# A decoder block on one core: when the last phase's weights are split, where its gate is applied, and where the head sums stand

## The chip, the core and the metric

The kernel runs on 1 core of one Trainium2 chip, in one launch. The metric is the device time of one execution in microseconds. The core has a matrix engine (TensorE, PE in the profile, with its weight loads as PEld), a vector engine (VectorE, DVE), a scalar engine (ScalarE, ACT), a general engine (GpSimd, POOL), and SyncE (SP), which here only issues transfers. Each engine works through its own queue in order. Transfers are issued from SP's queue (q1 in the profile) and from GpSimd's (q0), and run on sixteen DMA engines.

## What is computed

One decoder block with two parallel token mixers, over 2048 tokens of width 1024, all in float32:

```python
mod = silu(c) @ ada_w + ada_b                       # shift, scale, gate: 1024 each
h = rmsnorm(x, norm_g) * (1 + scale) + shift
p = h @ w_in                                        # 1024 -> 9344 columns
# branch A: GLU, causal depthwise convolution of width 31, layer norm over channels, swish
u = layernorm(conv(val * sigmoid(gate_c)), ln_g, ln_b)
y_conv = (silu(u) * silu(og_c)) @ w_conv_out
# branch B: RWKV-7 time mixing, 16 heads of 64
#   state = state * w - (state @ kk) kk*a + v k ;  o = state @ r
o = layernorm_per_head(o) + sum_head(r * k * r_k) * v
y_rwkv = (o * silu(og_r)) @ w_rwkv_out
m = sigmoid(g_conv) * y_conv + sigmoid(g_rwkv) * y_rwkv
x = x + gate * (m @ w_out)
return rmsnorm(x, final_g)
```

Three things of it bear on the change. `gate` multiplies a column of `m @ w_out`, so it can as well multiply that column of `w_out`. The layer norm needs one variance per token. And `sum_head(r * k * r_k)`, one number per token and head, is needed only when it multiplies `v`.

## The kernel before

**Blocks and phases.** The 2048 tokens are four blocks of 512. The first phase goes through them in order (loop `for b in range(NB)`, which builds `h`, the four `group`s, and the work between): the input projection, the convolution and the recurrence, whose results go to scratch in HBM. The last phase (the second loop over `b`) does the three output projections and the final norm. In the profile the first phase reaches until about 2570 us.

**Float32 by three products.** A float32 factor is split into a part `hi` in the format `F32R` and a rest `lo`. A projection is three matmuls per tile of 128 rows: `hi*hi`, `hi*lo`, `lo*hi` (`mm3k`, L173, and `part`, L1023 to L1025, for `w_out`).

**Weights.** `load_w` brings a weight tile of 128 x 1024 (512 KB) into a ring of six buffers, tag `w`. If `kept` holds the tile, two loads from GpSimd's queue fetch `hi` and `lo` from HBM scratch (L149, L150). Otherwise SP loads the tile (`w_st`, L153), ScalarE copies it to `hi` (L156) and VectorE or GpSimd subtracts (`lo`, L158). Only the tiles of `w_in` are stored back to be kept (`KEPT`), in block 0; blocks 1 to 3 load them split. The 24 tiles of `w_rwkv_out` (`ro`), `w_conv_out` (`co`) and `w_out` (`o`) are needed once in each block of the last phase, so they are split 96 times. There the rule of L157 gives every subtraction to VectorE.

**A group of the first phase.** `group(b, g, ...)` does four heads, as two `pair`s. A pair projects `k`, `r` and `v` (`shifted`), builds decay products, and forms the masked score tiles `As` (L504 on TensorE, L506 on VectorE). The tile `rk = r * k * r_k` is made on VectorE (L487); ScalarE copies its `hi` part (`rh`, L490), GpSimd subtracts the rest (`headsum`, L248), two matmuls sum it over the head (L249, L250), and ScalarE copies the sum back into `rk` (L492). All this stands ahead of the score tiles. `v` is projected after them, transposed (L519), and multiplied by `rk` on GpSimd (L522). Both `pv` and `pb` come from one ring of two PSUM buffers, tag `aux`. After both pairs comes a small inverse on GpSimd (L568, L570), fed by transfers `dA` and `dT` in SP's queue, and then the recurrence over eight chunks (L642 to L667). `fill` puts convolution and gate projections between. A scheduler that works on a model of the machine orders the instructions of each engine, by priority and program order; `tc.high_priority(HP)` raises a priority.

**The x buffers.** `hx(name)` gives a 128 x 512 buffer from a ring of four, tag `hx`. The next block's normalisation (`xnorm`), the loads of `h` (`hprep`, `hf`), and in block 3 the first block's layer norm and products (`lnorm_first`, `z_first`) use them.

**The gate.** In block 0, after group 0, `hgate_col` is filled: the gate, one column per 128 channels, times `0.5 * D`. Ahead of the last phase's loop, L986 to L992 turn it into rows: `grow`, the gate along the free axis in all 128 partitions, by eight diagonal tiles and matmuls against `ones` (which holds 1/1024).

**The last phase.** Block 0's branch projections (`rproj`, `cproj`) run beside the last recurrence. In the loop, block `b` has `cproj(b)`; then for the next block `osplit` (three loads, two products on GpSimd, a split) and `lnorm`; then the output projection, four column blocks `cb` of 256; then `rproj(b + 1)`. `lnorm` sums over channels with `ones` on TensorE, so that mean and variance stand in all 128 partitions (128 x 512); L969 and the nine steps of `rsqrt` (L123 to L128) work on that on VectorE, and GpSimd multiplies by it (L977). `addx` takes the products out of PSUM: VectorE multiplies by `grow` (`tg`, L1030), GpSimd adds to `x` (L1034; VectorE at the very end), ScalarE squares and sums (L1036). `finish` normalises and stores.

## Time and profile before

| | us |
|---|---|
| median of 3 runs | 3218.7 |
| lowest, highest | 3214.45, 3227.28 |
| the profiled execution | 3226.71 |
| its span, first to last instruction | 3225.0 |

The profile shows one execution. Busy time is that of an engine's own instructions; its share is of the span. "Idle before" in a row is the time in which the engine sat idle just before such an instruction, and behind `<-` stands what ended it. A window's row gives busy time and count of each engine, the clock that TensorE was granted (1.00 is full), the mean busy share of the sixteen DMA engines, and what they moved in GB/s. Matmuls are pipelined, so that a row's mean duration is longer than the distance from one to the next.

### The profile page before, as it was taken

To read this page: it belongs to the slowest core of one execution; us is meant where nothing else is said; L and a number is where in the kernel's file an instruction comes from. 1 tells how busy PE (TensorE), PEld (TensorE's weight loads), DVE (VectorE), ACT (ScalarE), POOL (GpSimd) and SP (SyncE) were. 2 spreads that over 40 slices of the span, in tenths; PEclk is the share of its full clock that TensorE was granted. 3 is DMA by queue.
4 is the path that set the end of the run, shared out by engine and by line. 5 is a ranking of instruction groups with operands and counts; after the bars stand their busy time and mean duration, and the time that the engine had idled before them with its cause. 6 is when DMAs were issued, how large, how long until landed. Compare 5 with 4: busy or idle time off the path is not lost.

```text
span 3225.0 us, 64867 instructions
## 1 busy us (share of the span) xinstructions
PE 3040.3 (94%) x25664; PEld 2832.5 (88%) x25664; DVE 2305.3 (71%) x4328; ACT 1062.0 (33%) x1900; POOL 1386.1 (43%) x2158
## 2 busy tenths in 40 slices
PE   6899999999999999899999998999989998688998
PEld 5899998989999999799999998999979888577887
DVE  6787777866676767575867676767788357999755
ACT  4432525241414132313232332222232323343422
POOL 3264444534343434343444435535546315655201
PEclk9999999999999999899999998999989999899999
DMA  7766666755565556364646676646537656655553
GB/s 292 260 238 226 229 218 244 230 176 157 161 185 157 168 179 192 113 186 145 191 151 184 185 217 183 196 134 193 158 108 242 206 183 203 219 177 182 171 166 121
DMA packets 328464, 606.95 MB, mean 188 GB/s; under 512 B 130848, under 2 KB 147552, under 8 KB 328160
## 3 DMA queue, kind: packets, MB, share of 16 engines
q1 hardware_dynamic: 265088, 373.14, 35.4%
q0 software_dynamic: 63072, 229.67, 23.2%
q8 instruction: 202, 3.31, 0.4%
q14 instruction: 102, 0.84, 0.1%
HBM read 439.03 MB, written 162.53 MB: 187 GB/s over the span
## 4 chain that ended last, share of the span: by engine, by line
PE 69%; DVE 14%; DMA 8%; issue 3%; POOL 3%; ACT 3%; SPq 1%; DVEq 0%; POOLq 0%; ACTq 0%
PE ps_main L173 47%; PE aux L504 3%; DMA w_st<-w_in_t 3%; PE xo L656 2%; PE xo L647 2%; PE xo L627 2%; PE xo L642 2%; PE pout L1024 2%; PE xo L662 2%; PE pout L1023 2%; PE pout L1025 2%; DVE acc L733 1%; DMA As<-dT 1%; ACT w_hi L156 1%; PE late L609 1%
## 5 line engine op out<-in xcount | busy, mean ns | idle before, releaser
L173 PE MATMUL ps_main<-h_hi,w_hi 128*128 128x256 f32 x4608 | 976.1, 289 | 15.3 <-DVE carry L401 9.1
L173 PE MATMUL ps_main<-h_lo,w_hi 128*128 128x256 f32 x4608 | 969.4, 287 | 0.2 <-DVE h_lo L328 0.2
L173 PE MATMUL ps_main<-h_hi,w_lo 128*128 128x256 f32 x4608 | 964.3, 287 | 3.2 <-POOL w_lo L158 3.0
L173 PEld LDWEIGHTS ps_main<-h_hi,w_hi 128*128 128x128 f32 x4608 | 725.8, 191 | 31.1 <-DVE carry L401 8.9
L173 PEld LDWEIGHTS ps_main<-h_lo,w_hi 128*128 128x128 f32 x4608 | 727.2, 191 | 9.4 <-issue 3.7
L173 PEld LDWEIGHTS ps_main<-h_hi,w_lo 128*128 128x128 f32 x4608 | 723.5, 191 | 13.1 <-POOL w_lo L158 4.0
L733 DVE SCALAR_TENSOR_TENSOR acc<-u,ck,acc 128x512 f32<-128x512 f32 x928 | 697.9, 752 | 23.5
L149 POOL DMA_DIRECT2D w_hi<-kh_in x219 | 126.2, 576 | 526.6 <-PE ps_main L173 497.0
L156 ACT CAST w_hi<-w_st 128x1024 fp32r<-128x1024 f32 x167 | 175.1, 1048 | 400.9 <-DMA w_st<-w_in_t 125.3
L158 DVE TENSOR_TENSOR w_lo<-w_st,w_hi 128x1024 fp32r<-128x1024 f32 x120 | 164.9, 1374 | 115.1 <-PE ps_main L173 45.2
L568 POOL TENSOR_TENSOR itmp<-La,TT 128x126 f32<-128x126 f32 (+22 forms) x496 | 181.0, 365 | 107.8 <-DMA La<-dA 75.4
L667 DVE SCALAR_TENSOR_TENSOR S<-xo,pe,Se 64x64 f32<-64x64 f32 x512 | 144.7, 283 | 93.1 <-PE xo L662 82.7
L637 ACT ACTIVATE Se<-S,pe 128x128 f32<-128x128 f32 x256 | 89.1, 395 | 357.9 <-DVE S L667 357.6
L570 POOL TENSOR_TENSOR TT<-TT,itmp 128x126 f32<-128x126 f32 (+22 forms) x496 | 189.6, 382 | 34.1
L506 DVE TENSOR_TENSOR As<-aux,maskA 128x512 f32<-128x512 f32 x128 | 88.1, 690 | 143.4 <-PE aux L504 142.7
L158 POOL TENSOR_TENSOR w_lo<-w_st,w_hi 128x1024 fp32r<-128x1024 f32 x47 | 112.9, 2401 | 112.9 <-ACT w_hi L156 89.2
L1034 POOL TENSOR_TENSOR xt<-xt,tg 128x256 f32<-128x256 f32 x60 | 55.5, 946 | 199.0 <-DVE tg L1030 196.5
L658 DVE TENSOR_TENSOR uv<-xo,rn 64x256 f32<-64x256 f32 x128 | 53.8, 421 | 120.5 <-PE xo L656 119.7
L504 PE MATMUL aux<-KR,BKz 128*128 128x128 f32 x1024 | 133.9, 277 | 1.9 <-DVE As L506 1.1
L522 POOL TENSOR_TENSOR vv<-rk,vv 128x512 f32<-128x512 f32 x32 | 45.0, 1407 | 197.5 <-PE aux L519 117.3
L504 PEld LDWEIGHTS aux<-KR,BKz 128*128 128x128 f32 x1024 | 123.7, 191 | 4.6 <-DVE As L506 1.8
L150 POOL DMA_DIRECT2D w_lo<-kl_in x219 | 119.3, 545 | 18.9 <-PE ps_main L173 11.1
(294 smaller groups left out, 5726.4 us busy)
## 6 DMA issues: line engine op xcount, KB each, us to landing
w_hi<-kh_in POOLq DMA_DIRECT2D x219, 512.0 KB, 4.1
w_lo<-kl_in POOLq DMA_DIRECT2D x219, 512.0 KB, 5.2
w_st<-w_in_t SPq DMA_DIRECT2D x73, 512.0 KB, 4.9
kh_in<-w_hi SPq DMA_DIRECT2D x71, 512.0 KB, 3.0
kl_in<-w_lo SPq DMA_DIRECT2D x71, 512.0 KB, 4.5
w_st<-w_ro_t SPq DMA_DIRECT2D x32, 512.0 KB, 4.1
w_st<-w_co_t SPq DMA_DIRECT2D x32, 512.0 KB, 3.6
w_st<-w_o_t SPq DMA_DIRECT2D x32, 512.0 KB, 3.6
```

Of the source, the lines that this page charges most:

```text
L149: nc.gpsimd.dma_start(hi, back[0])
L150: nc.gpsimd.dma_start(lo, back[1])
L156: nc.scalar.copy(hi, st)
L158: lo_eng.tensor_tensor(out=lo, in0=st, in1=hi.bitcast(F32), op=ALU.subtract)
L173: nc.tensor.matmul(ps[:, qs], ww[:, k, :], aa[k][:, qs], start=(k == 0 and t == 0 and q == 0), stop=(k == KT - 1 and t == 2 and q == ms - ...
L504: nc.tensor.matmul(pA[:, c // 2, es], BKz[:, hh, cc, es], KR[:, cc, es], start=(c == 0), stop=(c == 3), skip_group_check=True)
L506: nc.vector.tensor_tensor(out=Asb[:, hh, c4 * 4:c4 * 4 + 4, :].rearrange("p (a e) n -> p a (e n)", e=2), in0=pA, in1=flat(maskA).unsqueeze ...
L568: nc.gpsimd.tensor_tensor(out=tmp[:, :ni, :nt], in0=La[:, j:j + 1, j + 1:].broadcast_to([P, ni, nt]), in1=TT[:, :ni, j:j + 1].broadcast_to ...
L570: nc.gpsimd.tensor_tensor(out=TT[:, :ni, j + 1:], in0=TT[:, :ni, j + 1:], in1=tmp[:, :ni, :nt], op=ALU.add)
L637: nc.scalar.mul(Se[:, q, :], Sg[:, q, :], R[q]["pe"][:, c:c + 1])
L667: nc.vector.scalar_tensor_tensor(out=Sg[hs, q, hs], in0=xo[hs, 2 + q, hs], scalar=R[q]["pe"][hs, c:c + 1], in1=Se[hs, q, hs], op0=ALU.mult ...
L733: nc.vector.scalar_tensor_tensor(out=acc if i + 1 < HALO else yj, in0=u[:, i:i + TB], scalar=ck[:, j, i:i + 1], in1=acc, op0=ALU.mult, op1 ...
```

## The change

Five edits. (1) The 24 tiles of `ro`, `co` and `o` are split once, in halves of 128 x 512, behind the groups of blocks 1 and 2, three tiles to a group; the halves use the x buffers, the subtraction is GpSimd's, and both parts are stored in HBM scratch. In the last phase `load_w` then finds every tile kept. (2) The gate, times 0.5 alone, is stored to HBM as a row, and its 256 columns multiply a half of `o` before that is split; `grow`, its matmuls and the product in `addx` are gone, and `addx` is one addition on VectorE per token tile. (3) `lnorm` computes the variance with the tokens in the partitions, 128 x 4; `rsqrt` works on that, and four diagonal tiles and one matmul spread the result to 128 x 512. (4) In `pair` the head sums stand behind the transposes of `v`. (5) The two multiplications that take a branch projection out of PSUM, and the addition in `addx`, get the raised priority.

```diff
+    grow_d = dp.tile([D], F32, name="grow_d", tag="grow_d")
+    later = [(n, j) for n in ("ro", "co") for j in range(KT)] + [("o", (cb, kh)) for cb in range(4) for kh in range(2)]
...
+    def presplit(name, n, half):
...
+        hs = slice(half * 4, half * 4 + 4)
+        st, hi, lo = hx("w_st"), hx("w_hi"), hx("w_lo")
+        nc.sync.dma_start(st.rearrange("p (k n) -> p k n", k=4), wsrc[name][n][:, hs, :])
+        if name == "o":
+            gr = hx("w_gr")
+            nc.sync.dma_start(gr[:, :256], grow_d[n[0] * 256:n[0] * 256 + 256].unsqueeze(0).broadcast_to([P, 256]))
+            s4 = st.rearrange("p (k n) -> p k n", n=256)
+            nc.gpsimd.tensor_tensor(out=s4, in0=s4, in1=gr[:, :256].unsqueeze(1).broadcast_to([P, 2, 256]), op=ALU.mult)
+        nc.scalar.copy(hi.bitcast(F32R), st)
+        nc.gpsimd.tensor_tensor(out=lo.bitcast(F32R), in0=st, in1=hi, op=ALU.subtract)
+        for d_, s_ in zip(back, (hi, lo)):
+            nc.sync.dma_start(d_[:, hs, :].bitcast(F32), s_.rearrange("p (k n) -> p k n", k=4))
...
@@ pair
-        pb = pa.tile([P, TB], F32, name="aux", tag="aux")
-        rh = e1.tile([P, TB], F32R, name="rh", tag=RHT)
-        nc.scalar.copy(rh, rk)
-        headsum(pb, rk, rh)
-        nc.scalar.copy(rk, pb)
         yield
...
         for e in range(2):
             nc.scalar.copy(uv[vrow(e), e::2, q_, :], pv[vrow(e)])
+        pb = pa.tile([P, TB], F32, name="aux", tag="aux")
+        rh = e1.tile([P, TB], F32R, name="rh", tag=RHT)
+        nc.scalar.copy(rh, rk)
+        headsum(pb, rk, rh)
+        nc.scalar.copy(rk, pb)
         nc.gpsimd.tensor_tensor(out=vv, in0=rk, in1=vv, op=ALU.mult)
...
@@ first phase, behind a group
-                nc.vector.tensor_scalar(out=hgate_col, in0=hgate_col, scalar1=0.5 * D, scalar2=None, op0=ALU.mult)
+                nc.vector.tensor_scalar(out=hgate_col, in0=hgate_col, scalar1=0.5, scalar2=None, op0=ALU.mult)
+                nc.sync.dma_start(grow_d.rearrange("(n p) -> p n", p=P), hgate_col)
             wcount[0] = WDVE
             if todo:
                 fill(0, len(todo))
+            if b in (1, 2):
+                for _ in range(3):
+                    w_ = later.pop(0)
+                    for half in range(2):
+                        presplit(*w_, half)
...
@@ cproj, and alike in rproj
-            nc.vector.scalar_tensor_tensor(out=th, in0=th, scalar=1.0, in1=ppc, op0=ALU.add, op1=ALU.mult)
+            with tc.high_priority(HP):
+                nc.vector.scalar_tensor_tensor(out=th, in0=th, scalar=1.0, in1=ppc, op0=ALU.add, op1=ALU.mult)
...
@@ lnorm
-        pvar = pa.tile([P, TB], F32, name="pvar", tag="pvar")
-        nc.tensor.matmul(pvar, ones, qs, start=True, stop=True)
-        ve = t2("ve")
+        pvar = pa.tile([P, NTT], F32, name="pvar", tag="pvar")
+        for tt in range(NTT):
+            nc.tensor.matmul(pvar[:, tt:tt + 1], qs[:, tt * P:tt * P + P], ones[:, 0:1], start=(tt == 0),
+                             stop=(tt == NTT - 1), skip_group_check=True)
+        ve, rv = [b2.tile([P, NTT], F32, name=n_, tag=n_, bufs=1) for n_ in ("ve", "rv")]
         nc.vector.tensor_scalar(out=ve, in0=pvar, scalar1=LN_EPS, scalar2=None, op0=ALU.add)
+        rsqrt(rv, ve, b2, nc.vector)
+
+        dg = b2.tile([P, NTT, P], F32, name="dg", tag="ys", bufs=1)
+        for tt in range(NTT):
+            nc.vector.tensor_scalar(out=dg[:, tt, :], in0=ident, scalar1=rv[:, tt:tt + 1], scalar2=float(D),
+                                    op0=ALU.mult, op1=ALU.mult)
+        prl = pa.tile([P, NTT, P], F32, name="prl", tag="pmean")
+        nc.tensor.matmul(flat(prl), ones, flat(dg), start=True, stop=True)
         rl = b2.tile([P, TB], F32, name="rl", tag="rl", bufs=1)
-        rsqrt(rl, ve, b2, nc.vector)
+        nc.scalar.copy(rl, flat(prl))
...
@@ last phase: grow (L986 to L992) is taken out
-            def addx(t0, n, eng):
-                t_ = f2.tile([P, 2, 256], F32, name="tg", tag="tg")
-                nc.vector.tensor_tensor(out=t_[:, 0:n, :], in0=pts[t0 // 2][:, t0 % 2:t0 % 2 + n, :],
-                                        in1=grow[:, cs].unsqueeze(1).broadcast_to([P, n, 256]), op=ALU.mult)
-                for m in range(n):
-                    xt = xts[t0 + m][cb // 2][:, (cb % 2) * 256:(cb % 2) * 256 + 256]
-                    eng.tensor_tensor(out=xt, in0=xt, in1=t_[:, m, :], op=ALU.add)
+            def addx(t0):
+                xt = xts[t0][cb // 2][:, (cb % 2) * 256:(cb % 2) * 256 + 256]
+                with tc.high_priority(HP):
+                    nc.vector.tensor_tensor(out=xt, in0=pts[t0 // 2][:, t0 % 2, :], in1=xt, op=ALU.add)
...
```

`presplit`'s `back` is the pair of HBM scratch tiles that it puts into `kept`. `KEPT` is gone: `load_w` keeps whatever it splits, which after the change is `w_in` alone.

37 lines of the change are left out of this document (16 added, 21 removed).

## The prediction

> **What bounds the kernel now.** I read the page first, then the windows by stage, then TensorE's waits, and last the rows of the stage in which it waits.
>
> ```profile
> span 3225.0 us, 64867 instructions
> ...
> PE 3040.3 (94%) x25664; PEld 2832.5 (88%) x25664; DVE 2305.3 (71%) x4328; ACT 1062.0 (33%) x1900; POOL 1386.1 (43%) x2158
> ```
>
> TensorE is the bound, with 6% of idle time. The question is where those 185 us lie. In the next view the columns are window, its length, then busy time (count) of PE, PEld, DVE, ACT and POOL, granted clock, DMA share, GB/s.
>
> ```profile
> 700.00:1300.00 600.00, 590.19 (x5500) 561.12 (x5500) 418.22 (x831) 174.60 (x338) 242.62 (x487) 1.00 0.57 171
> 1300.00:1900.00 600.00, 585.21 (x5417) 557.90 (x5415) 419.64 (x859) 175.50 (x342) 252.04 (x495) 0.97 0.55 166
> ...
> 2570.00:2681.00 111.00, 107.36 (x567) 86.14 (x565) 62.01 (x99) 30.53 (x49) 14.44 (x10) 0.99 0.53 178
> 2681.00:3079.00 398.00, 343.64 (x1947) 298.44 (x1947) 325.62 (x428) 167.40 (x288) 213.78 (x152) 0.93 0.56 187
> 3079.00:3166.00 87.00, 87.00 (x387) 72.02 (x386) 49.35 (x100) 22.03 (x29) 1.43 (x2) 1.00 0.56 182
> 3166.00:3213.60 47.60, 46.68 (x386) 46.23 (x384) 20.67 (x45) 14.51 (x38) 8.64 (x12) 1.00 0.24 85
> 3213.60:3225.00 11.40, 0.00 (x0) 0.00 (x0) 7.77 (x35) 0.51 (x2) 0.00 (x0) 0.65 0.41 155
> ```
>
> The cuts follow the output projection's rows, of which the first and the last are these:
>
> ```profile
> L1023 PE MATMUL pout<-w_hi,o_hi x256: 277/281/552, 2680.9 to 3078.8; 128*128 128x256 f32 x128
> ...
> L1025 PE MATMUL pout<-w_hi,m_lo x256: 279/283/420, 2874.9 to 3213.3; 128*128 128x256 f32 x128
> ```
>
> Blocks 1 and 2 of the first phase (about 700 to 1900) run at 97 to 98%. The pressed stage is 2681 to 3079: three output projections and two pairs of branch projections. The last block shows what these cost undisturbed: 87.0 us for a pair, 47.6 us for an output projection, at full clock. So 3 x 47.6 + 2 x 87.0 = 317 us of work take 398 us: 81 us are lost to waits and to a clock of 0.93. The waits of TensorE, first those until 2570, then those after it (us, times, longest):
>
> ```profile
> PE aux L249 <- ACT rh L490: 37.7, 12, 9.1
> ```
> ```profile
> PE ps_main L173 <- DVE rs L123: 16.7, 2, 9.6
> PE ps_main L173 <- DVE w_lo L158: 15.2, 6, 4.6
> PE pout L1024 <- DVE w_lo L158: 8.6, 5, 2.5
> ...
> PE prow L991 <- DVE dg L990: 3.6, 2, 2.7
> ```
>
> Before 2570 one wait stands out, the head sums'. After it nearly all are for VectorE, which is 82% busy in the pressed stage.
>
> **Part A, head sums behind the v products.** The same two matmuls, two copies and one subtraction per pair are issued later; nothing is added. The 37.7 us are waits of L249 for `rh`, which waits for `rk` in VectorE's queue.
>
> ```profile
> 1300.00:1320.00 20.00, 10.86 (x98) 10.20 (x96) 19.13 (x49) 8.15 (x17) 11.03 (x13) 0.81 0.39 132
> 1320.00:1340.00 20.00, 20.00 (x230) 17.97 (x230) 8.18 (x18) 8.57 (x13) 5.31 (x8) 0.85 0.27 88
> ```
>
> Here, at the start of block 2, lies the longest, 9.1 us. VectorE is busy 19.1 of 20 us; the clock is 0.85 in the 20 us behind it, 3 us more. At four waits of this size for the 37.7 us, that makes 12 us: 50 us in all. The bounds are 0 (the wait changes hands) and -50. What is late next is VectorE again: the masks need L504, the transposes need `vv`, and `vv` stands right behind `rk` in that queue. In the changed program's order the transposes come before the head sums and the previous group's recurrence runs between them, so TensorE has other work at block starts, but it is work that VectorE feeds too. I take half, **-25 us**. The second transposed half of L530 now needs the PSUM buffer which the head sums hold until one more copy is done; projections stand around it, and bare it would be 32 copies of 0.6 us.
>
> The Trainium skill (TensorE: Matmul & The Clock Gate, HAM oscillation) says that a gap above about 3.4 us drops the clock to half until a busy window has passed. By that rule a long wait costs about 1.7 us more, an estimate, and Part A would be -22; the trace agrees in kind, and shows 3 us.
>
> **Part B, splitting 24 weights in blocks 1 and 2.** There are 48 halves, six behind each group. Each is one load, a ScalarE copy, a GpSimd subtraction and two stores; 16 also load the gate row and multiply on GpSimd. The nearest rows:
>
> ```profile
> L248 POOL TENSOR_TENSOR s_lo<-rk,rh 128x512 fp32r<-128x512 f32 x32 | 41.7, 1302 | 25.2 <-ACT rh L490 25.2
> ...
> L490 ACT CAST rh<-rk 128x512 fp32r<-128x512 f32 x32 | 19.8, 620 | 117.6 <-DVE rk L487 117.5
> ```
> ```profile
> L149 POOL DMA_DIRECT2D w_hi<-kh_in x219 | 126.2, 576 | 526.6 <-PE ps_main L173 497.0 <-issue 15.6 <-PE aux L504 10.8
> ...
> L150 POOL DMA_DIRECT2D w_lo<-kl_in x219 | 119.3, 545 | 18.9 <-PE ps_main L173 11.1 <-issue 3.6 <-PE xo L627 1.4
> ```
>
> GpSimd gets 64 x 1.30 = 83 us, over 1200 us in which it is busy 495; ScalarE gets 48 x 0.62 = 30 us beside 350. The stores and loads are 48 x 0.786 = 38 MB, about 113 us of all sixteen engines at 335 GB/s (worked out below), so the share goes from 0.56 to about 0.65. SP gets 160 issues in order: a store waits there for its subtraction, and behind it wait the stores of the gates, `dA` and the `hf` loads of the next block. The x buffers form one ring of four, so the next block's `hf` come behind the last halves. The cover is the slack of GpSimd's queue: it waits 497 us for TensorE before 219 weight loads, 2.3 us each, against 1.30 us for a subtraction. The bounds are 0 and 48 x 1.30 = 62 us, when each subtraction delays a weight by its full length. I take **+8 us**, near the covered end because of those 2.3 us.
>
> **Part C, the last phase.** All 96 weights of the last phase now come as two stored halves from GpSimd's queue. Gone are 96 ScalarE copies and 96 VectorE subtractions; w_out carries the gate, so the multiplication by `grow` and GpSimd's additions fall away for one VectorE addition per token tile. The reciprocal root goes from 512 to 4 columns, with a broadcast product and a ScalarE copy behind it. VectorE's rows in the pressed stage:
>
> ```profile
> L158 DVE TENSOR_TENSOR w_lo<-w_st,w_hi 128x1024 fp32r<-128x1024 f32 x55 | 81.8, 1488 | 28.4 <-ACT w_hi L156 12.9 <-PE pout L1024 12.5 <-PE ps_main L173 2.0
> L1030 DVE TENSOR_TENSOR tg<-pout,grow 128x512 f32<-128x512 f32 x23 | 15.6, 683 | 14.8 <-PE pout L1025 14.8
> ...
> L127 DVE SCALAR_TENSOR_TENSOR rs_t<-rs_t,ve 128x512 f32<-128x512 f32 x9 | 7.8, 865 | 0.1
> L126 DVE TENSOR_TENSOR rs_t<-rl 128x512 f32<-128x512 f32 x9 | 7.2, 798 | 0.2
> L128 DVE SCALAR_TENSOR_TENSOR rl<-rs_t,rl 128x512 f32<-128x512 f32 x9 | 7.2, 797 | 0.2
> ...
> L127 DVE SCALAR_TENSOR_TENSOR rs_t<-rs_t,gst 128x16 f32<-128x16 f32 x3 | 0.5, 176 | 0.1
> ```
> ```profile
> L1034 POOL TENSOR_TENSOR xt<-xt,tg 128x256 f32<-128x256 f32 x46 | 45.4, 1008 | 83.6 <-DVE tg L1030 83.5
> ```
>
> These take away 81.8 + 15.6 + 22.2 = 120 us. New are 48 additions, 0.34 us each if half of L1030's 0.683, and some 45 small ones at 0.18: 24 us. VectorE falls from 326 to 230 us, 73% of 317: it stops being what TensorE waits for. GpSimd loses 45 us and gains 55 x 1.12 = 62 us of issues: 231 us, no bound. But the eight normalising products (L977) stand in one row in its queue, and the weight loads behind them wait.
>
> The transfers are another matter. First the pressed stage's bytes and the weight loads among them, then the weight queue over blocks 1 and 2 (700 to 1900):
>
> ```profile
> q1 hardware_dynamic: 32759, 74.06, 55.6%
> ...
> w_st<-w_o_t SPq DMA_DIRECT2D x21, 512.0 KB, 3.8
> w_st<-w_ro_t SPq DMA_DIRECT2D x18, 512.0 KB, 4.0
> w_st<-w_co_t SPq DMA_DIRECT2D x16, 512.0 KB, 3.8
> ```
> ```profile
> q0 software_dynamic: 40320, 146.82, 39.9%
> ```
> ```profile
> 1880.00:1900.00 20.00, 20.00 (x182) 19.28 (x182) 17.95 (x36) 7.01 (x16) 3.18 (x6) 1.00 0.77 226
> 2420.00:2440.00 20.00, 20.00 (x183) 19.29 (x181) 18.04 (x31) 3.88 (x8) 14.56 (x33) 1.00 1.01 312
> ```
>
> At full share the first queue moves 74.06 MB / (0.556 x 398 us) = 335 GB/s, the second 146.82 / (0.399 x 1200) = 307 GB/s. In the stage 55 weights leave the first (28.8 of its MB), and come back as 57.7 MB on the second. So it takes 45.2/335 + 57.7/307 = 135 + 188 = 323 us of all sixteen engines, more than TensorE's 317. **The bound moves from VectorE to the transfers.** How full can they be held while TensorE works? TensorE was 20 of 20 us busy at shares of 0.77 and of 1.01. I take the middle, 0.9: 323/0.9 = 359 us, **-39**. The bounds are 323 us (-75) and 323/0.77 = 419 us (+21).
>
> From 2570 to 2681 the share is 0.53; 16 more weights raise 59 us of transfers to 89 of 111, 0.80: **+2** (0 to 5). After 3079, 24 weights raise 60 us to 104 of 135: 0.77, nothing. The `prow` matmuls and their 3.6 us of waiting fall away: **-4**. The tail of 11.4 us stays but for one short operation. The small store of the gate row and the copies of ada's columns lie in block 0 beside projections: nothing; bare it would be one transfer of about 3 us.
>
> **Sum:** -25 + 8 - 39 + 2 - 4 = -58. The profiled execution took 3226.7 us (span 3225.0), so 3169. The median of the runs shown is 3218.7, 8 lower, so **3161 us**, with 3135 to 3190 from A and C at a quarter of their bounds.
>
> **Rivals.** (1) *The transfers don't bind.* Then the stage comes to about 330 us (-68) and Part A gives -40, B nothing: -112, **3107**. For it: 1.01 beside a full TensorE at 2420. Against: that lasted 20 us, and the stage is 320. The Trainium skill (DMA: Bandwidth & Descriptors, Specifications) puts a core's HBM limit at about 358 GB/s; by that, an estimate, the stage's 103 MB need 287 us and this rival holds. The row at 2420 shows 312 GB/s at a full share, less than that; the first queue alone, at the start, moved more:
>
> ```profile
> 20.00:40.00 20.00, 15.36 (x109) 13.82 (x108) 18.20 (x40) 8.03 (x12) 4.17 (x3) 1.00 1.03 410
> ```
>
> (2) *The head sums' wait changes hands.* The v products hang on the same VectorE queue 1 us later. A is 0: -33, **3186**. For it: VectorE at 96% at that place. Against: the order puts other work between.
>
> (3) *Slower: the splits hold up the weights of blocks 1 and 2.* A subtraction that waits for its own load or for a ring buffer stands in GpSimd's queue ahead of the next weights, and TensorE has 2% of slack there. If each half costs 2.5 us (the subtraction twice over), that is 120 us: -58 - 8 + 120 = +54, **3273**. It decides from 66/48 = 1.4 us per half on. Against: the 2.3 us of slack per weight.
>
> (4) *The transfers hold at 0.77.* Stage +21, 2570 to 2681 +5, so -25 + 8 + 21 + 5 - 4 = +5: **3224**, no change. For it: 0.77 is the fuller of the longer stretches. The stage loses from a share of 323/398 = 0.81 downwards.
>
> That the splits stay in the last phase can be excluded: the changed program has no copy or subtraction of a w_out, w_ro or w_co tile there.
>
> **Chances.** Forecast 0.38, (1) 0.17, (2) 0.20, (3) 0.12, (4) 0.13. Less than 0.5% (16 us) can't be told from no change. Faster: the first two and nine tenths of (2), 0.73; same: a tenth of (2), most of (4), 0.14; slower: (3) and a little of (4), 0.13. The range from 3098 to 3224 leaves out (3), the worse half of (4), and the better end of (1).
>
> **What would show it.** Right: no VectorE wait above 10 us in total for L173 after 2681, the stage near 359 us at a share of 0.9, weight loads that land later than 5 us; `aux L249` with less than half of its 37.7 us; blocks 1 and 2 still above 96%. Wrong: a share below 0.8 with the stage still long (then GpSimd's queue or VectorE binds), the stage near 320, or projections in blocks 1 and 2 waiting for `w_hi` loads.

## The result, and the profile after

The changed kernel is slightly slower: 3243.0 us median of 22 executions against 3229.3 of the kernel before, ratio 1.0047 with a 95% interval of 1.0034 to 1.0059. The forecast was 3161. The profiled execution's span is 3241.7 us, 16.7 more than before. From the page of the changed kernel, its span and the engines' busy time:

```profile
span 3241.7 us, 65210 instructions
...
PE 3056.1 (94%) x25672; PEld 2841.8 (88%) x25672; DVE 2117.6 (65%) x4260; ACT 993.9 (31%) x1855; POOL 1492.9 (46%) x2354
```

VectorE lost 188 us of work, GpSimd gained 107, and TensorE stands where it stood. The next view of the changed kernel has its windows, with the columns as before. The first four are blocks 0 to 3, cut at the first projection of the next block's `h` and, for the last, at the end of block 3's projections; the fifth is the pressed stage, from the first output projection to the end of the third.

```profile
0.00:704.27 704.27, 619.18 (x5445) 585.68 (x5445) 501.85 (x971) 262.40 (x435) 303.50 (x425) 0.95 0.66 227
704.27:1317.41 613.14, 602.24 (x5498) 574.48 (x5497) 412.41 (x863) 198.05 (x380) 283.64 (x525) 0.99 0.66 200
1317.41:1956.06 638.65, 614.75 (x5634) 585.03 (x5633) 425.84 (x885) 195.98 (x380) 300.81 (x532) 0.98 0.65 197
1956.06:2595.12 639.06, 623.11 (x5742) 587.68 (x5740) 444.35 (x882) 184.82 (x333) 336.67 (x566) 0.98 0.63 191
2719.70:3095.90 376.20, 340.04 (x1966) 293.96 (x1965) 235.74 (x418) 115.00 (x237) 210.64 (x218) 0.94 0.83 281
```

The kernel before, its four blocks cut the same way:

```profile
0.00:649.89 649.89, 596.74 (x5244) 566.88 (x5245) 494.41 (x934) 256.54 (x423) 299.16 (x423) 0.97 0.70 243
649.89:1271.40 621.51, 607.79 (x5635) 577.80 (x5633) 435.54 (x886) 186.06 (x358) 255.43 (x502) 0.99 0.57 170
1271.40:1898.65 627.25, 611.52 (x5634) 581.86 (x5633) 435.90 (x893) 185.76 (x360) 255.43 (x502) 0.98 0.56 168
1898.65:2555.77 657.12, 627.48 (x5816) 593.21 (x5815) 464.59 (x893) 191.31 (x344) 337.60 (x555) 0.97 0.60 182
```

It ends block 0 at 649.9 us and block 3 at 2555.8 (the last recurrence goes on beside the first branch projections, until 2675), and its pressed stage takes 398.3. So the four blocks lose 39.3 us together, and the pressed stage wins 22. The waits of TensorE in the changed kernel (us, times, longest):

```profile
PE ps_main L195 <- ACT w_hi L182: 20.1, 5, 10.1
...
PE ps_main L195 <- DVE mr L955: 15.7, 2, 8.0
PE late L622 <- DVE T L618: 14.7, 9, 2.8
PE ps_main L195 <- DVE u_lo L905: 11.7, 5, 4.8
PE ps_main L195 <- DVE th L737: 11.1, 3, 8.2
...
PE aux L271 <- DVE As L523: 0.3, 1, 0.3
```

The 37.7 us in front of the head sums are gone (L271 is the old L249). In their place `w_in`'s splits in block 0 (L182), tiles of the small inverse, transposed on VectorE (`T`, for which the kernel before has no row), and a gate (`th`) are late. In the last phase VectorE is still late, for `mr` and `u_lo`, though it works 236 us there and not 326.

### The profile page after: what moved, and what is told of

It is laid out like the page before. It is cut to its first block, busy times and chain, and to the rows that moved or that the text cites. A ratio compares the mean times of both kernels' runs of the same rounds, so it can differ in the third digit from the quotient of the medians.

```text
span 3241.7 us, 65210 instructions
## 1 busy us (share of the span) xinstructions
PE 3056.1 (94%) x25672; PEld 2841.8 (88%) x25672; DVE 2117.6 (65%) x4260; ACT 993.9 (31%) x1855; POOL 1492.9 (46%) x2354
## 4 chain that ended last, share of the span: by engine, by line
PE 61%; DMA 14%; DVE 11%; issue 5%; POOL 4%; ACT 3%; SPq 1%; POOLq 0%; DVEq 0%; ACTq 0%
PE ps_main L195 42%; PE aux L521 3%; DVE acc L755 3%; DMA w_st<-w_in_t 2%; PE xo L678 2%; PE xo L649 2%; PE xo L669 2%; DMA w_gr<-grow_d 2%; DMA As<-dT 2%; PE xo L664 2%; PE xo L684 2%; PE pout L1053 1%; DMA dT<-TT 1%; PE pout L1054 1%; PE pout L1052 1%
## 5 line engine op out<-in xcount | busy, mean ns | idle before, releaser
L680 DVE TENSOR_TENSOR uv<-xo,rn 64x256 f32<-64x256 f32 x128 | 53.9, 421 | 151.6 <-PE xo L678 150.7
L182 ACT CAST w_hi<-w_st 128x1024 fp32r<-128x1024 f32 x71 | 74.4, 1047 | 189.4 <-DMA w_st<-w_in_t 126.7
L672 DVE COPY X<-xo 64x256 f32<-64x256 f32 x128 | 53.8, 421 | 100.9 <-PE xo L669 99.4
L664 PE MATMUL xo<-S,KR 128*128 128x128 f32 x512 | 98.7, 283 | 8.6 <-DVE S L689 5.9
```

The lines of the kernel that those rows point to most:

```text
L664: nc.tensor.matmul(xo[:, q, :], R[q]["KR"][:, cc, es], Sg[:, q, :], start=(q == 0), stop=False, skip_group_check=True)
```

## The experiments

All in one table. The ratio is of medians to the kernel before, with its interval; the other columns are from each kernel's trace: the end of block 0 and of block 3, and the length of the pressed stage, cut as above. Kernels with the changed kernel's first phase unaltered (e8, e9, e11, e16) end block 3 at 2599 to 2603, the changed kernel's own profile at 2595: differences of less than some 8 us mean nothing here.

| kernel | ratio | block 0 | block 3 | stage |
|---|---|---|---|---|
| before | 1 | 650 | 2556 | 398 |
| changed | 1.0047 (1.0034 to 1.0059) | 704 | 2595 | 376 |
| e1, changed, head sums back | 1.0062 (1.0041 to 1.0083) | 656 | 2592 | 396 |
| e2, before + head sums moved | 0.9992 (0.9971 to 1.0013) | 702 | 2566 | 398 |
| e3, changed, gate row in 512 B pieces | 1.0030 (1.0011 to 1.0049) | 697 | 2588 | 378 |
| e4, before, all weights kept | 1.0028 (1.0006 to 1.0049) | 649 | 2560 | 407 |
| e5, before + head sums, b > 0 | 0.9978 (0.9965 to 0.9991) | 650 | 2550 | 402 |
| e6, changed, head sums for b > 0 only | 1.0152 (1.0135 to 1.0169) | 657 | 2612 | 392 |
| e7, changed, no gate | 1.0041 (1.0018 to 1.0064) | 705 | 2599 | 384 |
| e8, changed, one final root | 1.0075 (1.0043 to 1.0106) | 703 | 2599 | 383 |
| e9, changed, high parts alone | 1.0132 (1.0089 to 1.0174) | 706 | 2602 | 394 |
| e10, changed, halves moved only | 0.9987 (0.9966 to 1.0008) | 700 | 2547 | 398 |
| e11, changed, short sums | 1.0101 (1.0056 to 1.0145) | 703 | 2603 | 391 |
| e12, e5 + column variance | 0.9975 (0.9954 to 0.9996) | 647 | 2554 | 396 |
| e13, changed, copies on GpSimd | 1.0062 (1.0038 to 1.0085) | 706 | 2602 | 381 |
| e14, changed, subtractions on VectorE | 1.0055 (1.0035 to 1.0075) | 700 | 2599 | 378 |
| e15, before + head sums but the first group's | 0.9981 (0.9966 to 0.9996) | 647 | 2558 | 398 |
| e16, changed, own `mr` buffers | 1.0069 (1.0049 to 1.0090) | 700 | 2601 | 385 |
| e17, changed, copies alone | 1.0047 (1.0018 to 1.0076) | 709 | 2567 | 396 |
| e18, changed, subtractions alone | 0.9998 (0.9964 to 1.0032) | 706 | 2575 | 379 |

### Taking the change apart: e1 to e4

e1 puts the head sums of the changed kernel back ahead of the first `yield`; e2 is the reverse edit on the kernel before:

```diff
+        pb = pa.tile([P, TB], F32, name="aux", tag="aux")
+        rh = e1.tile([P, TB], F32R, name="rh", tag=RHT)
+        nc.scalar.copy(rh, rk)
+        headsum(pb, rk, rh)
+        nc.scalar.copy(rk, pb)
         yield
...
-        pb = pa.tile([P, TB], F32, name="aux", tag="aux")
...
         nc.gpsimd.tensor_tensor(out=vv, in0=rk, in1=vv, op=ALU.mult)
```

e3, on the changed kernel, stores the gate row in eight pieces of 512 bytes for 1024 of 4; e4, on the kernel before, keeps all split weights:

```diff
-                nc.sync.dma_start(grow_d.rearrange("(n p) -> p n", p=P), hgate_col)
+                nc.tensor.transpose(hgt, hgate_col, ident)
+                nc.scalar.copy(hgr, hgt)
+                nc.sync.dma_start(grow_d.rearrange("(n p) -> n p", p=P), hgr)
```
```diff
-KEPT = ("in",)
+KEPT = ("in", "ro", "co", "o")
```

> The changed kernel with the head sums back ahead of the score tiles; all else stays changed. Theory H (the moved head sums cost the first block): the 40 us that the changed kernel loses up to about 700 us come back, the first block ends within 15 us of the kernel before, L249's wait of some 30 us is there again, and the time falls below the kernel before, to about 3205. Rival S (the store of the gate row and what the scheduler makes of it costs the first block): block 0 stays 30 to 40 us late and the time is 3240 or more.

> The kernel before with the head sums moved and nothing else. Theory H: the first block ends 30 to 40 us later than before, the time is about 3250 to 3265. Rival S: the first block is unchanged, L249's wait of 37.7 us is mostly gone, and the time is 3195 to 3215.

> The changed kernel with the gate columns turned on TensorE and stored as 8 rows of 512 bytes in place of 1024 pieces of 4 bytes. Theory G (the pieces hold up the weight load issued just before them, 12 us to land instead of 5): the 10 us wait at 146 us falls to 2 or 3, and the time falls by 8 to 14 us, to about 3230. If the store has no part in it, the wait stays and the time is 3243 within 5.

> The kernel before, which now keeps every weight that it splits, so that the last phase splits 24 tiles in its first block and loads them split in the others: no work in blocks 1 and 2, gate and variance as before. If taking the splits off VectorE is what shortens the last phase: the stretch from the second output projection to the end falls by 15 to 25 us, and the time is 3205 to 3215. If the stretch is held by the transfers or by the normalising steps in VectorE's queue: within 5 us of the kernel before.

The head sums are what block 0 pays for: it takes 702 to 704 us with them moved and 650 to 656 with them in place, whatever else is changed. e2's median of 3231 us fits neither of its two theories, because its later blocks are shorter (more on that below). In e1 the wait for the sums is back with 18.5 us, and yet e1 is no faster than the changed kernel, so the splitting costs as much without the move: blocks 0 to 3 end at 2592 for 2556. And e1, whose last phase is the changed kernel's, needs 396 us for the pressed stage, no less than before. Storing the gate row in large pieces (e3) halves the wait behind the old store, from 10.1 to 5.0 us, but moves the ratio by less than the intervals tell. In e4 the last phase splits each weight once and then reads both parts back. Its pressed stage:

```profile
2687.90:3094.40 406.50, 343.77 (x1948) 301.57 (x1948) 246.33 (x373) 118.99 (x237) 237.71 (x251) 0.91 0.80 271
```

VectorE has 246 us of work there for the 326 of before, and the stage is 8 us longer; the stretch from the second output projection on, which was to lose 15 to 25 us, takes 7 more. VectorE's amount of work alone does not set its length; e4 also moves 110 MB in the stage for 74, which e9 below looks at.

### Where the head sums cost: e5, e6, e15

The five lines stand at both places, under a condition: `b > 0` in e5 (on the kernel before) and e6 (on the changed kernel), `b > 0 or pr > 1` in e15 (on the kernel before; pairs 0 and 1 are the first group).

```diff
+        if not (b > 0):
+            pb = pa.tile([P, TB], F32, name="aux", tag="aux")
...
         yield
...
+        if b > 0:
+            pb = pa.tile([P, TB], F32, name="aux", tag="aux")
...
         nc.gpsimd.tensor_tensor(out=vv, in0=rk, in1=vv, op=ALU.mult)
```

> The kernel before with one part of the change, and that in three blocks of four: the head sums stand behind the v products for b > 0, while block 0 keeps them ahead of the score tiles. Theory D (the move gains in the blocks with a full cover and costs in the first, which also splits and stores w_in): block 0 takes the 650 us of before instead of the 702 of the run with the sums moved everywhere, blocks 1 to 3 the 605, 612 and 647 of that run; about 3184 profiled, ratio 0.987. Rival (the gain of blocks 1 to 3 in that run was only work of block 0 done late, so it is gone with the loss): blocks 1 to 3 take their 622, 627 and 657 of before, ratio 1.00.

> The kernel before with the head sums moved everywhere but in the first group of block 0. In the run with all sums moved the projections are 189 matmuls behind at 280 us (1205 for 1394 of before) and 207 behind at 720 us, so the loss arose in the first group, 80 to 280 us. Theory D1: without it block 0 takes 650 to 656 us and blocks 1 to 3 keep 605, 612 and 647; ratio 0.990 to 0.993. Rival (the waits change hands whatever group is moved): blocks 0 to 3 end at 2550 to 2556 as with the sums moved for b > 0, ratio 0.998.

Block 0's loss arises in its first group. The window from 80 to 280 us, of the kernel before, of e2 and of e15, in this order:

```profile
80.00:280.00 200.00, 185.92 (x1602) 175.95 (x1603) 153.22 (x266) 76.66 (x118) 93.02 (x139) 0.97 0.71 243
```
```profile
80.00:280.00 200.00, 174.18 (x1425) 163.57 (x1425) 140.87 (x247) 70.66 (x110) 80.53 (x111) 0.89 0.62 208
```
```profile
80.00:280.00 200.00, 187.48 (x1604) 178.10 (x1605) 154.72 (x269) 77.37 (x118) 96.60 (x149) 0.96 0.72 245
```

With the first group's sums moved, 177 matmuls fewer run in these 200 us, at a clock of 0.89 and a lower DMA share; with only that group left alone (e15) nothing is lost. But the second half of theory D (e5) and of D1 (e15) did not come true. Blocks 1 to 3 were to take 605, 612 and 647 us as in e2; they take 613, 627 and 660 in e5 and 624, 620 and 667 in e15. e2's short blocks were the other face of its long block 0, since its projections lagged by 200 matmuls and the recurrence did not. What the move is worth without the first group, in the ends of block 3, is -5 and +2 us, as e15's rival had it. The wait has changed hands: in e5's waits of TensorE a row is new,

```profile
PE ps_main L173 <- ACT ta L437: 18.3, 3, 11.5
```

for `ta`, a tile of a pair which ScalarE makes ahead of `rk`.

> The changed kernel, with the head sums moved for b > 0 alone. Theory D: block 0 falls from 704 to about 652, the other stages stay as in the changed kernel (613, 639, 639), except that the 13 us of work that block 0 did for the next come back in block 1; about 3200 profiled, ratio 0.991 to 0.995. Rival (block 0 is slow by the extra tiles and the gate column's store and not by the head sums): block 0 stays above 690, ratio above 1.00.

Block 0 does fall to 657, but block 2 rises to 685, and e6 is the slowest of all. ScalarE's waits in its block 2 (1268 to 1953 us) show where:

```profile
ACT w_hi L164 <- POOL w_st L163: 106.2, 14, 13.2
```

That is the copy of a half of `w_out`, which stands in ScalarE's queue until GpSimd has the gate's columns and has multiplied; in the changed kernel the same row has 53.9 us. So the gate can cost much, where the order is unlucky.

### What the splitting costs: e7, e10, e13, e14, e17, e18

All are edits of `presplit` in the changed kernel. e7 leaves out the gate, and e10 the copy and the subtraction too:

```diff
-        if name == "o":
-            gr = hx("w_gr")
...
-        nc.scalar.copy(hi.bitcast(F32R), st)
-        nc.gpsimd.tensor_tensor(out=lo.bitcast(F32R), in0=st, in1=hi, op=ALU.subtract)
-        for d_, s_ in zip(back, (hi, lo)):
+        for d_ in back:
...
```

e13 and e14 keep the gate and change the engine of one operation each:

```diff
-        nc.scalar.copy(hi.bitcast(F32R), st)
+        nc.gpsimd.tensor_copy(hi.bitcast(F32R), st)
```
```diff
-        nc.gpsimd.tensor_tensor(out=lo.bitcast(F32R), in0=st, in1=hi, op=ALU.subtract)
+        nc.vector.tensor_tensor(out=lo.bitcast(F32R), in0=st, in1=hi, op=ALU.subtract)
```

e17 is e7 without the subtraction, and e18 is e7 without the copy:

```diff
-        nc.gpsimd.tensor_tensor(out=lo.bitcast(F32R), in0=st, in1=hi, op=ALU.subtract)
-        for d_, s_ in zip(back, (hi, lo)):
+        for d_, s_ in zip(back, (hi, st)):
```
```diff
-        nc.scalar.copy(hi.bitcast(F32R), st)
-        nc.gpsimd.tensor_tensor(out=lo.bitcast(F32R), in0=st, in1=hi, op=ALU.subtract)
-        for d_, s_ in zip(back, (hi, lo)):
+        nc.gpsimd.tensor_tensor(out=lo.bitcast(F32R), in0=st, in1=st, op=ALU.subtract)
+        for d_, s_ in zip(back, (st, lo)):
```

> The changed kernel, in which each half of the 24 tiles is loaded in blocks 1 and 2 and stored twice, but not split: ScalarE's copies, GpSimd's subtractions and the gate are left out, so the weights and the output are not the reference's. The cost of the halves in blocks 1 and 2 was 34 us against the run with the sums alone (613 and 639 us against 605 and 612). Theory Q (copies and subtractions stand in ScalarE's and GpSimd's queues and wait there for their loads, with the recurrence's copies behind them): blocks 1 and 2 fall to about 608 and 615. Theory M (the transfers themselves, and the x buffers that they hold, cost it): they stay near 613 and 639.

> The changed kernel, with the halves of w_out split without the adaLN gate: the broadcast load of the gate row and its product with the weights are left out, so the output lacks the gate. Theory G (block 2 lost its 26 us because the halves of w_out wait for the gate's load, 54 us on ScalarE in 12 waits, with later weight casts queued behind): block 2 falls from 639 to 612 to 620, ratio about 0.997. Rival (the mere splitting of 12 tiles, 24 halves of copies, subtractions, loads and stores in each block costs it): block 2 stays above 630, ratio above 1.001.

Blocks 1 and 2 of e10:

```profile
699.91:1302.88 602.97, 600.01 (x5499) 572.44 (x5497) 408.65 (x869) 183.84 (x356) 252.57 (x501) 0.99 0.67 204
1302.88:1923.32 620.44, 610.71 (x5635) 581.25 (x5633) 419.35 (x891) 186.62 (x358) 253.82 (x502) 0.99 0.66 200
```

All the weights' transfers are there (share 0.67 and 0.66, as in the changed kernel), and TensorE is idle for 12.7 us of two blocks against 34.8. The traffic costs nothing that shows; the 48 us between e10 and the changed kernel come with the splitting. 28 of them lie in blocks 1 and 2, and 16 in block 3, which has no halves to split. They are not the gate's: without it (e7) block 2 stays at 642 us and the blocks end at 2599.

> The changed kernel, with both the rounding copy and the subtraction of each presplit half on GpSimd, none on ScalarE. Before it, moving the halves without splitting them ended blocks 0 to 3 at 2547 us, the changed kernel at 2595: 48 us are the splitting's. Theory S (ScalarE's in-order queue: its copies of halves wait for loads and gates, 54 us in block 2, and the recurrence's copies stand behind them): the blocks end near 2560. Theory P (GpSimd's queue: the recurrence's products and the kept weights' issues stand behind the subtractions and the gate): they end at 2595 or later, since GpSimd has more to do.

> The changed kernel, with the subtraction of each presplit half on VectorE and not on GpSimd; the copies stay on ScalarE and the gate's product on GpSimd. Theory S: the blocks end at 2590 or later, since ScalarE still waits and VectorE has 48 operations more. Theory P: they end near 2570.

Both came out at the no-gain end (2602 and 2599): a copy or a subtraction costs about the same on another engine. So these two could not name a queue, and the last two left work out instead of moving it.

> The changed kernel, with ScalarE's copies of the presplit halves alone: the subtraction and the gate are left out and the unsplit half is stored in the place of the low part, so the output is not the reference's. Blocks 0 to 3 ended at 2547 us with the halves moved and nothing computed, and at 2599 with copy and subtraction but no gate. Theory S2 (the copy in ScalarE's queue costs it, wherever the subtraction runs): they end at 2580 or later. Theory P2 (GpSimd's subtraction does): 2550 to 2560. Theory B2 (each of the two engines' operations costs its part): 2565 to 2580.

> The changed kernel, with GpSimd's subtractions of the presplit halves alone: the copy and the gate are left out, the unsplit half is stored in the place of the high part and taken from itself for the low part, so the output is not the reference's. Theory P2 (GpSimd's subtraction costs the 52 us): blocks 0 to 3 end at 2580 or later. Theory S2 (ScalarE's copy): 2550 to 2560. Theory B2 (each its part): 2565 to 2580.

Copies alone end the blocks at 2567 and subtractions alone at 2575, 20 and 28 us behind e10, and both together (e7) 52, as theory B2 had it. This is not yet proof that each costs its part: in blocks 1 and 2, where the halves are, the three differences are 14, 18 and 40 us, and e10 itself ends 20 us before e2, which has no halves at all. The changed kernel's rows between 704 and 1956 us show that a half takes up more than its duration (POOL's rows, then ACT's; behind the bar the idle time in front of them):

```profile
L165 POOL TENSOR_TENSOR w_lo<-w_st,w_hi 128x512 fp32r<-128x512 f32 x48 | 61.8, 1287 | 59.2 <-ACT w_hi L164 58.1 <-DMA La<-dA 0.8
L163 POOL TENSOR_TENSOR w_st<-w_st,w_gr 128x512 f32<-128x512 f32 x16 | 20.7, 1294 | 51.5 <-DMA w_gr<-grow_d 51.3
```
```profile
L164 ACT CAST w_hi<-w_st 128x512 fp32r<-128x512 f32 x48 | 29.7, 618 | 109.3 <-POOL w_st L163 53.9 <-DMA w_st<-w_co_t 28.9 <-DMA w_st<-w_ro_t 22.5
```

A half holds GpSimd's queue for (61.8 + 59.2 + 20.7 + 51.5) / 48 = 4.0 us, and ScalarE's for 2.9, where their operations alone last 1.3 to 2.6 and 0.6. At one place the trace shows what that does. TensorE's longest wait in blocks 1 and 2 is 8.2 us, from 1934.2 to 1942.4, for a gate's product (`th`, L737). ScalarE's timeline just before (start, duration; in brackets the idle time in front):

```profile
1938.80 0.62 ACT L164 CAST w_hi<-w_st 128x512 fp32r<-128x512 f32 x1 [8.84 <-POOL w_st L163]
1939.44 0.37 ACT L651 COPY uv<-xo 64x256 f32<-64x256 f32 x1
1939.83 0.60 ACT L735 ACTIVATE th<-ps_main 128x512 f32<-128x512 f32 x1
```

ScalarE stood for 8.84 us at a half's copy, which waited for GpSimd's product and that for the gate's load; the recurrence's copy and the gate's own operation stood behind it. But this is one wait. e7 has none like it in block 2 (none above 3.0 us), and costs as much.

A rival stays untested. The experiments that leave work out also leave out x buffers and waits of SP. A half takes three or four of the four x buffers in the changed kernel, three in e7, two in e17 and e18, and one in e10. And a half's stores stand in SP's queue until its parts are made, in the changed kernel's blocks 1 and 2 above all here:

```profile
SPq L167 <- ACT w_hi L164: 155.5, 36, 8.5
```

Added up from the traces, SP waits in front of these stores for 199 us in blocks 1 and 2 of the changed kernel, 192 in e7, 140 in e17, 155 in e18 and 27 in e10, and for 226 and 214 in e13 and e14, which change the engine alone. The ends of the blocks (2595, 2599, 2567, 2575, 2547, 2602, 2599) go with these waits, and nearly so with the buffers, at least as well as with the engines' work. So it is shown that splitting the halves costs the time and moving them does not; which queue or ring it goes through is not shown.

### What sets the pressed stage: e8, e9, e11, e12, e16

Four are edits of the changed kernel: e9 (`load_w`), e11 (`lnorm`; the squares of the other tiles go too), e8 (behind the output projection) and e16 (`mnew`). e12 is e5 with the changed kernel's lines from `pvar` to `rl` in `lnorm`, and the raised priority in `cproj` and `rproj`.

```diff
             nc.gpsimd.dma_start(hi, back[0])
+            if name != "in":
+                return hi, hi
```
```diff
-            if j:
-                nc.gpsimd.tensor_tensor(out=ys, in0=ys if j > 1 else y[0], in1=yj, op=ALU.add)
+            if j == 1:
+                nc.gpsimd.tensor_tensor(out=ys, in0=y[0], in1=yj, op=ALU.add)
...
-            if j:
-                nc.gpsimd.tensor_tensor(out=qs, in0=qs, in1=sq, op=ALU.add)
```
```diff
-            for tt in range(NTT):
-                finish(tt)
+            with tc.high_priority(HP):
+                vs = f2.tile([P, NTT], F32, name="vs", tag="vs")
+                nc.vector.tensor_reduce(out=vs, in_=sq4, axis=AX.X, op=ALU.add)
...
+                rsqrt(rs, vs, f2, nc.vector)
...
```
```diff
-        return [oa.tile([P, TB], F32, name=f"mr{n}", tag=f"mr{n}") for n in range(KT)]
+        return [oa.tile([P, TB], F32, name=f"mr{n}", tag=f"mo{n}" if n < 3 else f"mr{n}") for n in range(KT)]
```

> The changed kernel, with only the high halves of the kept ro, co and o weights read back in the last phase, and used in the place of the low halves too, so the output lacks their low parts. That leaves out half of the 106 MB that the stage from the first output projection to the last but one moves, about 40 MB. Theory T (transfers set the pace of that stage, as the prediction had it): the three output stages, 176, 153 and 137 us, shrink together by 60 us or more. Theory E (the elementwise chain of the next block's normalization and the two waits for mr set it): they shrink by less than 20 us together, and the waits for u and mr stay.

> The changed kernel, with GpSimd's sums over the eight tiles in the last phase's layer normalization cut to the first two tiles for the mean and the first for the variance, so that normalization is another: it leaves out six and seven GpSimd additions in each block, about 18 us of 128x512 operations, and seven squares on ScalarE. Theory E (the elementwise chain sets the pace of the output stages): the first two output stages fall by 8 us or more each. Theory T (transfers): they stay within 4 us of 176 and 153.

The pressed stage of e9:

```profile
2728.90:3122.80 393.90, 341.32 (x1966) 295.52 (x1966) 238.90 (x393) 111.98 (x229) 178.87 (x162) 0.93 0.59 192
```

The stage moves 76 MB for 106 (30 less, not the 40 of the expectation), the share falls from 0.83 to 0.59, and the stage takes 394 us for 376. Transfers do not set its pace. Theory E found no support either: with less to sum (e11), the first output stage, from one block's output projection to the next's, grows from 176 to 193 us, and the second stays at 152. So each of the two theories had an experiment against it, though what e11 was to gain, 16 us, is less than the scatter shown further down.

> The changed kernel, with the last normalization's reciprocal square root of the four token tiles in one pass over four columns instead of four passes over one, and ahead in priority. Theory F (the two waits of 8 us for mr in the last phase, and the low clock behind them, come from VectorE's queue, where the 11 tiny operations of four tiles and the centring of y stand ahead of the eviction): both waits fall below 3 us, the first two output stages lose 8 to 12 us each, ratio about 0.999. Rival (the eviction waits for the store of the finished rows, whose buffer it takes over): the waits stay above 5 us, ratio 1.003 to 1.006 as for the changed kernel.

> The changed kernel, with buffers of their own for the first three of the eight mr tiles, which otherwise take over those of the finished rows. Theory B1 (the eviction of the first projections waits until VectorE has finished and stored the rows whose buffers it takes, hence the two waits of 8 us): both waits fall under 3 us and the first two output stages lose 8 us or more each from 176 and 153. Rival (the eviction stands behind the centring of y in VectorE's order anyway): the waits stay over 5 us each.

> The kernel before with the two parts of the change that touch no weights: the head sums behind the v products for b > 0, and the variance per token in a column with the projections' evictions at high priority. Theory E (what the last phase won came from the shorter chain on VectorE): the three output stages fall from 194, 161 and 133 by 10 us or more together, ratio about 0.994. Theory R (what it won came from reading split weights back): they stay as in the kernel with the sums alone, ratio 0.998.

The wait for `mr` in the changed kernel, as VectorE's timeline shows it (start, duration); TensorE stood still from 2780.8 to 2788.8:

```profile
2779.78 1.41 DVE L1073 SCALAR_TENSOR_TENSOR xt<-xt,rs,fg 128x512 f32<-128x512 f32 x2
...
2781.24 4.86 DVE L991 TENSOR_TENSOR y<-y,pmean 128x512 f32<-128x512 f32 x8
...
2786.34 1.77 DVE L905 TENSOR_TENSOR o_lo<-ot,o_hi 128x512 fp32r<-128x512 f32 x1
2788.03 0.67 DVE L955 SCALAR_TENSOR_TENSOR mr<-rth,ps_main 128x512 f32<-128x512 f32 x1
```

The eviction, the product that takes a projection out of PSUM (L955, 0.67 us), stands behind eight centrings (the subtraction of the mean, L991) and a split. The buffer that it writes to held a finished row, whose store landed at 2783.6 by the trace; so nearly 3 us of the wait had to be, and 4.4 us are the order's. One root for four tiles (e8) left the two waits at 20.3 us in all, and buffers of its own (e16) at 11.0: neither below the 3 us each that the theories asked for. The column variance and the priorities alone (e12) shorten the stage by 6 us against e5, and the three output stages by 4 together where theory E asked for 10; the ratio stays (0.9975 for 0.9978).

One comparison is stronger than these. Ten kernels have the changed kernel's last phase, instruction for instruction, and differ only in the first. Their pressed stages take 376 (changed), 378 (e3), 378 (e14), 379 (e18), 381 (e13), 384 (e7), 392 (e6), 396 (e1 and e17) and 398 us (e10). Counted from the traces, e18's VectorE does the stage's 417 operations in exactly the changed kernel's order, and so do its other three engines with theirs, and its stage is 3 us longer; in e1, e10 and e17 only 84 to 88% of them stand in the same order, and the stage takes 20 us more. The share alone doesn't tell the time (e7 keeps 88% too, and takes 384): it matters which ones change places. A scatter of 22 us is as much as e4 and e11 were to show; of the experiments on this stage only e9, with its 60 us or more, asked for clearly more than it. Two of the ten, e18 first, then e10:

```profile
2698.50:3077.90 379.40, 341.37 (x1966) 294.89 (x1965) 235.24 (x418) 114.71 (x237) 209.09 (x218) 0.94 0.83 279
```
```profile
2676.60:3074.10 397.50, 346.67 (x1966) 298.21 (x1965) 248.34 (x418) 114.49 (x237) 206.26 (x218) 0.92 0.80 266
```

Same counts, nearly the same work; 18 us apart.

Of the versions that leave nothing out, e5, e12 and e15 are the ones whose interval lies below both kernels, below the kernel before by 0.2% each, at the edge of what can be told.

## Why the prediction was wrong

In the profiled executions the sum can be redone by parts, with e2 between the two kernels. A: 2566.4 - 2555.8 = +11 at the end of block 3 (forecast -25). B: 2595.1 - 2566.4 = +29 (forecast +8). C: behind block 3, 646.6 for 669.2 us, -23 (forecast -39 + 2 - 4 = -41). Together +17, as the spans have it. All three terms were off the same way, by 75 us; the median from which the forecast started, 3218.7, was 11 us below that of 22 runs. With e1 as the kernel in between the shares are others (the splits and the last phase first: +36 and -4; then the sums: +4 and, behind block 3, -19), because each edit orders the queues anew. The signs of A and B at the end of block 3 are the same both ways; most of C's gain is missing in e1.

**Part A: the removed wait was real, its worth wasn't.** "I take half, -25 us" is the step that failed. The rows of L249 vanished as foreseen, to 0.3 us, far below half. What the step called late next, "VectorE again", came with others: the wait changed hands, which was rival (2), and the gain is between -5 and +2 us where block 0's first group is left alone. The loss in that group was not foreseen: I argued from the start of block 2 alone, and block 0 also splits and stores `w_in`; up to the end of block 3 TensorE's waits for such splits (`w_hi`) are 17.3 us in e2 and 2.2 before. Without the move of that group the loss is gone (e15). Which of its instructions is the late one was not tried.

**Part B: the duration was right, the price wasn't.** A subtraction lasts 1.287 us (1.302 forecast), a copy 0.618 (0.620), and the DMA share rose to 0.66 and 0.65, as forecast. The step "near the covered end because of those 2.3 us" is the one that failed: it set the slack per weight against the duration of a subtraction alone. With what a half waits for in the queue it holds GpSimd 4.0 us and ScalarE 2.9, and that is past the 1.4 us from which rival (3) decides. The place was wrong too: the step looked for the cost at the weights behind GpSimd's queue, and in the changed kernel TensorE never waits for a stored part of `w_in` (none of its rows of waits has `w_hi<-kh_in` or `w_lo<-kl_in`). Its largest waits in blocks 1 and 2 are for `T` (11.3 us in 7) and `th` (8.2 in one). Where the cost goes through stays open: work taken off GpSimd (e14) or ScalarE (e13) gained nothing, and the work left out in e10, e17 and e18 took x buffers and waits of SP with it. The test "blocks 1 and 2 still above 96%" held (98 and 96%) and showed nothing, since block 2 grew by 11 us with it. e10 ends the blocks 20 us before e2, although it does more; that may be order too, and it leaves B between 29 and 48 us.

**Part C: the amount of work was right, the bound wasn't.** VectorE's 230 us came out as 236, GpSimd's 231 as 211, the transfers' 323 us of all sixteen engines as 0.83 x 376 = 312; the stored parts landed later than 5 us at the median (`kl_o` at 6.6), but for `kh_co` (4.1). "It stops being what TensorE waits for" and "The bound moves from VectorE to the transfers" failed. The waits for VectorE stayed (15.7 and 11.7 us, where none above 10 was to be), and with the traffic at 0.59 the stage was no shorter. e9 shows that the DMA engines' sum does not set the stage; e4 speaks against VectorE's sum, within the scatter. The ten kernels show that the same instructions take 376 to 398 us, and the same order nearly the same time. So what stretches the stage's 317 us of TensorE work is, as far as the runs tell, what stands in front of what in the queues. The 22 us gained belong to one order of the same instructions; another gains 1. Why one order is better, beyond the two places of `mr`, stays open.

**Rivals.** (2) holds for A. The sign of (3) holds for B, at 29 to 48 us and not 120; its mechanism, late weights in blocks 1 and 2, does not show. (1) and (4) were both about transfers that do or don't bind; these don't bind, and the stage still didn't come to 330. With 0.13 on slower and 0.14 on no change, the chances were wrong by more than the sum: three separate terms each had a bound on the bad side, and the rivals let only one of them go bad at a time.

## What to carry to other kernels

A share of 82% for an engine is not yet a bound: before costing a stage by one engine's or the DMA engines' sum, look at what stands ahead of the late instruction in its queue, and ask whether the edit changes that. Price work that is added to an in-order queue by its duration plus the wait that it brings along, its stores and its buffers included, and not by its duration. Where a scheduler orders the queues anew at each edit, that alone moved a stage here by 20 us with the same instructions, so a forecast gain below that can't be read from the edit.

## What the runs showed of the hardware

VectorE's operations on one column were not always short. In the changed kernel's pressed stage (VectorE's groups; busy time, mean ns):

```profile
L905 DVE TENSOR_TENSOR u_lo<-y,u_hi 128x512 fp32r<-128x512 f32 x24 | 24.4, 1018 | 2.8 <-ACT u_hi L904 2.7
L127 DVE TENSOR_TENSOR rs_t<-rs 128x1 f32<-128x1 f32 x27 | 18.0, 673 | 0.0
...
L991 DVE TENSOR_TENSOR y<-y,pmean 128x512 f32<-128x512 f32 x24 | 14.7, 677 | 0.0
```

In the row of L127 one element per partition costs as much, on average, as 512 in that of L991. The timeline of one of them, VectorE first, then GpSimd:

```profile
2769.23 3.27 DVE L127 TENSOR_TENSOR rs_t<-rs 128x1 f32<-128x1 f32 x1
2772.43 0.14 DVE L124 TENSOR_SCALAR rs<-vs 128x1 int32<-128x1 int32 x1
```
```profile
2769.24 1.30 POOL L986 TENSOR_TENSOR ys<-ys,y 128x512 f32<-128x512 f32 x1
2770.49 1.29 POOL L925 TENSOR_TENSOR ot<-ot,rt 128x512 f32<-128x512 f32 x1
2771.73 0.59 POOL L175 DMA_DIRECT2D w_hi<-kh_ro  x1
```

It lasts through two GpSimd operations and into the issues behind them. The centring (L991), which has one operand in PSUM, keeps its 677 ns throughout, while the split (L905), with both in SBUF, averages 1018. Counted from the trace, the 17 of L127's 27 that have no GpSimd operation beside them last 0.15 to 0.16 us, and the ten others 1.56 on average. The Trainium skill (SBUF — State Buffer, SBUF: two separate sides) has VectorE operations with two SBUF inputs and GpSimd operations that read SBUF take turns on one pair of ports, held for a whole instruction. The trace agrees: 3.27 us for a column beside GpSimd, 0.15 for the shortest without it. So GpSimd's work lengthens VectorE's, which my durations from single rows left out.
